# Block sums of x made early, and one VA/GA pair moved from plain chunks to block products

## The chip, the cores and the metric

The kernel runs on one core of one Trainium2 chip. The metric is the device time of one execution in microseconds. The core has TensorE (PE, matrix products into PSUM), VectorE (DVE), ScalarE (ACT), GpSimd (POOL) and SyncE (SP). ACT, POOL and SP issue the DMA transfers, most of them SP.

## The reference, cut to what matters

One decoder layer on x of 1024 positions by 1024 channels, in float32. The input projection has 56 column blocks of 128: VA and GA (8 each), XB and GB (12 each), SA and SB (8 each).

```python
h = rms_norm(x, g_mix)
z = einsum("bsd,de->bse", h, w_in) + b_in          # 1024 x 7168
va, ga, xb, gb, sa, sb = split(z)
u = va * sigmoid(ga)
u = causal_depthwise_conv(u, conv_a_w, conv_a_b)   # 31 taps
u = silu(layer_norm(u)); y_a = u @ w_a_out
v = causal_depthwise_conv(xb, conv_b_w, conv_b_b)  # 4 taps
v = rg_lru(v, ...)                                 # 16 heads, gates, scan along positions
y_b = (v * gelu(gb)) @ w_b_out
m = sigmoid(sa) * y_a + sigmoid(sb) * y_b
x = x + m @ w_o
h = rms_norm(x, g_mlp); x = x + square(relu(h @ w_1)) @ w_2
return rms_norm(x, g_final)
```

## The kernel before, in words

**Arithmetic.** Each float32 operand is split into a high part h rounded to fp32r and a low part l, the rest. A product is three matmuls: h·h, h·l and l·h. All matmuls spoken of here have a 128x128 weight and a 128x512 moving operand. There are two ways to make the parts. `split` has ACT copy h and DVE subtract to get l. `split_dma` (L64) has ACT write l = −src (L66), then POOL issues a DMA that adds src to l (L67, an accumulate), and ACT writes h = src (L68): the low part is ready when that transfer lands, and DVE has no part in it.

**Opening** (chunks 0 to 2). x is loaded, normalised and scaled into eight tiles `xc` of 128x1024, and split into `xh` and `xl`. The columns of x and of time are arranged as a 2x2 block matrix for part 2; `xc[i]` holds one half of a block.

**Part 1**, `for s in range(3, NC1)`: one chunk per step, that is one column block of `w_in` against all of x, 48 matmuls (`chunk_mm`, L724, matmul at L735). The order of the column blocks is the list `CH`: all 12 XB blocks and all 8 pairs VA, GA, 28 chunks. `w_load(s + 2)` puts the 512 KB load of a coming chunk on SP's queue, `w_parts(s + 1)` splits the next chunk's weights with `split_dma`. The chunk reads h of the weights in its first 32 matmuls and l in the last 16. Among chunk matmuls stand those of the recurrence's heads (`head_mm`). After each chunk ACT and DVE finish its column block: `xb_out` for XB, `u_out` (L583) for a VA/GA pair: ACT's sigmoid of GA and one DVE multiply of 1024 columns; `u` then feeds the 31-tap convolution. The recurrence's elementwise work comes in groups of three tiles: `scan_exp` (ACT), `scan_in` (DVE), `scan_root` (ACT), `scan_tile` (DVE, with a store to `hd`).

**Part 2** does the other column blocks in pairs (`ZPAIRS`, 14 pairs: 6 GB, 4 SA, 4 SB) by a 2x2 block scheme with seven products instead of eight. Product p of pair i is 12 matmuls (`z_mm`, L925, matmul at L933) of a left operand made from the weights (`z_lhs`, L769, out of sums of weight blocks by `z_sums`) and a right operand `xbh[p]`, `xbl[p]`. For p = 1, 2, 3 the right operand is a part of x itself; for p = 4, 5, 6, 7 it is a sum of blocks of x, split. Five of the seven left operands are split with `split_dma`, two with ACT and DVE. Products are combined in PSUM: ACT copies a bank on to another bank, and the next product adds to it. `z_bank` (L918) gives such a bank; where it says so, a first matmul into the bank comes ahead (the opening matmul, L922), for banks b and e of the first two pairs. `z_out` (L938) finishes a column block: for GB gelu and a product with the recurrence, for SA and SB a sigmoid, stored to DRAM. `zseq` is the order of all products; the loop over n takes step n of it, with left operands made four steps ahead, weight sums five ahead and weight loads (`ZL`) further ahead. `ZX` lists extra work by step.

**The sums of x.** At s = 3 eight stores write `xc` to the DRAM tensor `xu`. At s = 23 and s = 25 `x_load` (L669) reads four tiles each back on SP's queue, `x_sum` (L676) makes four differences each on DVE one chunk later, and `x_parts` (L681) splits them at s = 25 to 27 and in part 2 just ahead of step 0 and at steps 0, 2 and 4: six tiles by ACT and DVE, two (p = 5 and 4 of the first column half) by `split_dma`.

**What sets the order.** Parts 1 and 2 are under `tc.manual_schedule`: the order of each engine's instructions is the order in which the code issues them. `later` collects DVE work with a due time, and `vector_work` issues it sorted by that time and fills the spare time with convolution taps (`fill`, 0.67 us each), by a clock of planned costs (`clk["P"]`, `clk["A"]`, `clk["V"]`). SP, POOL and ACT work off their queues in order, so a transfer that waits for a tile holds up what stands behind it. Tiles come from pools with a fixed number of buffers: `tp` (tag T, 37 tiles of 128x1024) for most, `qp` (tag p, 4) for weight tiles and head tiles, `ep` (tag e) for one x tile. Part 2's last step is followed by the b stage (L1121), which needs the product of recurrence and gelu, and later by the sum over the convolution's tiles.

Of the kernel before, what the change touches and what calls it, by code (L numbers as in the profile page):

```python
# [9 lines left out]
F32 = mybir.dt.float32  # L10
# [21 lines left out]
def trunk_kernel(ctx: ExitStack, tc: tile.TileContext, x, xt_in, xt_eo, vecs, w_in, w_a_out, w_b_out,  # L32
# [87 lines left out]
    ep = stage.enter_context(tc.tile_pool(name="extra", bufs=1))  # L120
# [285 lines left out]
    xu = dp.tile([2, 4, P, S], F32, name="xu")  # L406
# [75 lines left out]
    def xb_parts(t):  # L482
        if t % 3 == 2:
            vp_[t] = tuple(qp.tile([P, S], F32R, tag="p", name=f"vt{x}{t}", bufs=4) for x in "hl")
        else:
            vp_[t] = T(f"vth{t}", F32R), T(f"vtl{t}", F32R)
# [64 lines left out]
    def scan_exp(g):  # L551
        at("A", 1.28)
        for t in range(3 * g, 3 * g + 3):
# [113 lines left out]
    xq = {}  # L667

    def x_load(c2):  # L669

        xq[c2] = {n: ep.tile([P, S], F32, tag="e", name=f"xs{n}_{c2}") if (n, c2) == (21, 0) else T(f"xs{n}_{c2}")
                  for n in (11, 12, 22, 21)}
        for n, a in xq[c2].items():
            nc.sync.dma_start(a, xu[n % 10 - 1, 2 * (n // 10 - 1) + c2])

    def x_sum(c2, ready):  # L676
        q = xq[c2]
        for n, a, b in ((11, 12, 11), (12, 22, 12), (22, 22, 11), (21, 21, 22)):
            later(ready, 1.2, nc.vector.tensor_tensor, q[n], q[a], q[b], ALU.subtract)

    def x_parts(c2, *ps):  # L681
        for p in ps:
            src = xq[c2][{6: 22, 7: 12, 5: 11, 4: 21}[p]]
            xbh[p][c2] = h = T(f"xs{p}h_{c2}", F32R)
            xbl[p][c2] = l = T(f"xs{p}l_{c2}", F32R)
            if c2 == 0 and p < 6:
                split_dma(src, h, l)
                at("A", 2.0)
            else:
                nc.scalar.activation(h, src, AF.Copy)  # L690
                later(at("A", 1.0), 1.2, nc.vector.tensor_tensor, l, src, h.bitcast(F32),
                      ALU.subtract)

    CH = [XB, VA, GA, XB + 1, XB + 2]
    for js, g in (((1,), 1), ((2,), 2), ((3,), 3), ((4, 5, 6, 7), 4)):
        CH += [c for j in js for c in (VA + j, GA + j)]
        CH += [XB + t for t in range(3 * g, min(3 * g + 3, 12))]
# [41 lines left out]
    ZPAIRS = [GB + 2 * i for i in range(6)] + [SA + 2 * i for i in range(4)]  # L739
    ZPAIRS += [SB + 2 * i for i in range(4)]  # L740
# [4 lines left out]
    def z_load(i, kk):  # L745

        zraw[i, kk] = raw = qp.tile([P, 2, 4, P], F32, tag="p", name=f"zw{i}_{kk}", bufs=4)
        c = ZPAIRS[i]
        nc.sync.dma_start(raw, w_in[c:c + 2, :, 4 * kk:4 * kk + 4, :].rearrange("m p k c -> p m k c"))
# [52 lines left out]
    HS0 = [4 + 5 * (n // 4) + n % 4 for n in range(NH)]  # L802
    head_at = {s: n for n, s in enumerate(HS0)}

    EXP = {head_slot: g for g, head_slot in enumerate(HS0[4 * g + 3] + 1 for g in range(4))}
    XL = {23: 0, 25: 1}
    XS = {25: ((x_parts, 0, 6),), 26: ((x_parts, 0, 7, 5),), 27: ((x_parts, 0, 4),)}
# [3 lines left out]
    for c2 in range(4):  # L811
        nc.sync.dma_start(xu[1, c2], xc[4 + c2])
    w_parts(3)
    with tc.manual_schedule(engines=ENGINES):
        for s in range(3, NC1):
            w_load(s + 2)
            if s in XL:
                x_load(XL[s])
# [19 lines left out]
            if before is not None:  # L838

                head_gate(before, 0, begun)  # L840
                head_mm(before, 1)
            if s > 3:
                chunk_mm(s, 18, 24)
            if new is not None:
# [20 lines left out]
            for d in range(6):  # L865
                if s - d in EXP:
                    g = EXP[s - d]
                    lag = int(g < 3)
# [9 lines left out]
                    if 3 * g <= t < 3 * g + 3 and t < 11:  # L878
                        later(rooted[t], 4.8, scan_tile, t)
            if s == NC1 - 1:  # L880
                z_get(0, z_lhs)
                z_get(1, z_lhs)
            if s - 1 in XL:
                x_sum(XL[s - 1], max((r for r, *_ in todo), default=0))
# [1221 lines left out]
```

## Time and profile before

| | |
|---|---|
| median of 3 runs | 1548.86 us (1547.82 to 1549.61) |
| profiled execution | 1549.04 us, span 1547.2 us |
| granted TensorE clock | 0.998 |
| PE busy | 1535.6 us (99%) |
| weight loads of PE busy | 1264.6 us (82%) |
| DVE busy | 1214.5 us (78%) |
| ACT busy | 903.6 us (58%) |
| POOL busy | 188.6 us (12%) |
| part 1, 33 to 360.5 us | PE busy 327.5 of 327.5, DMA share 0.60 |
| part 2, 360.5 to 630 us | PE busy 269.34 of 269.5, DMA share 0.93 |

The span runs from the first to the last instruction; the rest of an execution's time lies around it. Busy times of matmuls are modelled ends of pipelined instructions, so the difference of two starts tells more than a length. The DMA share is the mean busy share of the 16 DMA engines and can read a little over 1. In rows of a timeline the columns are start, duration, engine, line, operation, output<-inputs, and in brackets the idle time ahead with what ended it. In rows of a list of waits they are who waited for what, the total, how often, and the longest. In rows of a table by stretch they are busy time of PE, its weight loads, DVE, ACT and POOL with counts, then clock, DMA share and GB/s. In rows of DMA issues they are the tiles, the queue, the count, KB each and the median time from issue to landing.

### The profile page before, as it was taken

To read this page: it belongs to the slowest core of one execution; us is meant where nothing else is said; L and a number is where in the kernel's file an instruction comes from. 1 tells how busy PE (TensorE), PEld (TensorE's weight loads), DVE (VectorE), ACT (ScalarE), POOL (GpSimd) and SP (SyncE) were. 2 spreads that over 40 slices of the span, in tenths; PEclk is the share of its full clock that TensorE was granted. 3 is DMA by queue.
4 is the path that set the end of the run, shared out by engine and by line. 5 is a ranking of instruction groups with operands and counts; after the bars stand their busy time and mean duration, and the time that the engine had idled before them with its cause. 6 is when DMAs were issued, how large, how long until landed. Compare 5 with 4: busy or idle time off the path is not lost. (4 is left out here: it accounts for less than half of the span.)

```text
span 1547.2 us, 19086 instructions
## 1 busy us (share of the span) xinstructions
PE 1535.6 (99%) x6804; PEld 1264.6 (82%) x6804; DVE 1214.5 (78%) x1641; ACT 903.6 (58%) x1266; POOL 188.6 (12%) x226
## 2 busy tenths in 40 slices
PE   9999999999999999999999999999999999999998
PEld 7878888788888888888888887888888888888886
DVE  6999989999899983468568868765555558888897
ACT  6748677576667667435375777545444475555553
POOL 0000000002222222000022322000000001111110
PEclk9999999999999999999999999999999999999999
DMA  8653554678999889854579978523333779888852
GB/s 348 169 127 95 160 140 134 158 227 214 264 267 256 195 206 259 270 196 126 185 195 306 194 171 198 211 75 124 113 115 111 242 216 229 226 223 223 205 124 109
DMA packets 124943, 294.18 MB, mean 190 GB/s; under 512 B 12464, under 2 KB 30512, under 8 KB 124848
## 3 DMA queue, kind: packets, MB, share of 16 engines
q1 hardware_dynamic: 93312, 213.00, 40.7%
q0 software_dynamic: 31392, 79.71, 28.1%
q8 instruction: 53, 0.87, 0.2%
q14 instruction: 42, 0.34, 0.1%
q10 hardware_dynamic: 144, 0.26, 0.1%
HBM read 152.93 MB, written 58.72 MB: 137 GB/s over the span
## 5 line engine op out<-in xcount | busy, mean ns | idle before, releaser
L735 PE MATMUL z<-xh,win_h 128*128 128x512 f32 x400 | 125.0, 390 | 0.0
L735 PE MATMUL z<-xl,win_h 128*128 128x512 f32 x400 | 123.5, 390 | 0.0
L1873 DVE TENSOR_TENSOR acc<-acc,d 128x1024 f32<-128x1024 f32 x72 | 87.8, 1220 | 33.4 <-PE d L1861 32.7
L735 PE MATMUL z<-xh,win_l 128*128 128x512 f32 x400 | 99.4, 391 | 0.0
L735 PEld LDWEIGHTS z<-xh,win_l 128*128 128x128 f32 x400 | 75.2, 188 | 16.8
L735 PEld LDWEIGHTS z<-xh,win_h 128*128 128x128 f32 x400 | 75.1, 188 | 16.5 <-ACT win_h L68 0.4
L648 DVE SCALAR_TENSOR_TENSOR y<-u,vec,y 128x511 f32<-128x511 f32 (+14 forms) x120 | 88.5, 737 | 0.0
L735 PEld LDWEIGHTS z<-xl,win_h 128*128 128x128 f32 x400 | 75.1, 188 | 15.8
L648 DVE SCALAR_TENSOR_TENSOR yt<-u,vec,yt 128x511 f32<-128x511 f32 (+6 forms) x112 | 82.6, 737 | 0.0
L648 DVE SCALAR_TENSOR_TENSOR y<-yt,csum,y 128x511 f32<-128x511 f32 (+6 forms) x112 | 82.6, 737 | 0.0
L542 ACT ACTIVATE g<-rg,vec 96x1024 f32<-96x1024 f32 x32 | 35.6, 1113 | 79.6 <-PE rg L532 79.6
L1540 ACT ACTIVATE o<-s 128x512 fp32r<-128x512 f32 x58 | 34.7, 623 | 52.8 <-DVE s L1525 31.3
L67 POOL DMA_DIRECT2D win_l<-win_raw x25 | 21.6, 865 | 319.1 <-ACT win_l L66 248.4
L476 DVE SCALAR_TENSOR_TENSOR v<-xb,vec,v 128x1023 f32<-128x1023 f32 (+2 forms) x36 | 46.2, 1282 | 11.4 <-ACT v L467 10.4
L67 POOL DMA_DIRECT2D zo<-zw x42 | 36.2, 862 | 133.6 <-ACT zo L66 125.3
L1121 PE MATMUL yb<-hgl,wb_h 128*128 128x512 f32 x168 | 51.8, 390 | 0.0
L1121 PE MATMUL yb<-hgh,wb_h 128*128 128x512 f32 x168 | 51.8, 389 | 0.0
L66 ACT ACTIVATE zo<-zw 128x512 fp32r<-128x512 f32 x42 | 26.3, 626 | 30.7 <-DMA zw<-in_w_in_dram 8.7
L67 POOL DMA_DIRECT2D db_1l<-wr x7 | 6.0, 860 | 309.8 <-DMA wr<-in_w_dram 254.0
L1121 PE MATMUL yb<-hgh,wb_l 128*128 128x512 f32 x168 | 41.0, 390 | 0.0
L1085 DVE TENSOR_TENSOR o<-s,o 128x512 fp32r<-128x512 f32 x58 | 38.8, 682 | 0.0
L1121 PEld LDWEIGHTS yb<-hgh,wb_h 128*128 128x128 f32 x168 | 31.6, 188 | 6.5
(1795 smaller groups left out, 4672.9 us busy)
## 6 DMA issues: line engine op xcount, KB each, us to landing
w_raw<-in_w_dram SPq DMA_DIRECT2D x36, 512.0 KB, 5.5
fr<-fd SPq DMA_DIRECT2D x32, 512.0 KB, 5.9
wr<-in_w_dram SPq DMA_DIRECT2D x32, 512.0 KB, 6.5
zw<-in_w_in_dram SPq DMA_DIRECT2D x28, 512.0 KB, 5.9
win_raw<-in_w_in_dram SPq DMA_DIRECT2D x25, 512.0 KB, 4.1
win_l<-win_raw POOLq DMA_DIRECT2D x25, 512.0 KB, 4.5
zo<-zw POOLq DMA_DIRECT2D x42, 256.0 KB, 5.6
gates<-zg SPq DMA_DIRECT2D x32, 256.0 KB, 4.0
```

Of the source, the lines that this page charges most:

```text
L66: nc.scalar.activation(l, src, AF.Copy, scale=-1.0)
L67: nc.gpsimd.dma_start(l, src, accum_op=ALU.add)
L476: nc.vector.scalar_tensor_tensor(v[:, d:S], a[:, 0:S - d], cbw_c[:, w * 12 + t:w * 12 + t + 1], v[:, d:S], ALU.mult, ALU.add)
L542: nc.scalar.activation(a, gps.pop((n, gi))[:HD, :], AF.Sigmoid, bias=(ba_c, bx_c)[gi][:, n:n + 1])
L648: nc.vector.scalar_tensor_tensor(o[:, k:], a[:, 0:HS - k], c, o[:, k:], ALU.mult, add)
L735: nc.tensor.matmul(zps[s][:, HALVES[hf]], w[:, k, :], xw[k][part][hf], start=n == 0, stop=n == 23)
L1085: tt(l, src, h.bitcast(F32), ALU.subtract)
L1121: nc.tensor.matmul(ps[hf], a, b[:, HALVES[hf]], start=n == 0, stop=n == len(todo) - 1)
L1540: nc.scalar.activation(o[:, 0], src, AF.Copy)
L1873: tt(acc[p, q2], acc[p, q2], ps, ALU.add)
```

## The change

- The sums of x are made in place in `xc`, at s = 4 and s = 6 (`x_sum`). `x_make` at s = 5 to 7 splits those for p = 6 and 7 at once into high and low parts and has them written to the DRAM tensor `xsd` (the high part by a DMA that ACT issues, the low part by SP in `x_store`); those for p = 4 and 5 are written as they are. The eight early stores of plain x are gone; there are twelve later ones.
- `x_get` at s = 24 and 25 loads both parts for p = 6 and 7 (eight loads). `x_raw` at steps 0 and 4 of part 2 loads the sums for p = 5 and 4 (four loads), and `x_split` at steps 2, 3, 6 and 7 splits them by ACT and DVE.
- VA7 and GA7 leave part 1, which has 26 chunks (`CH` is written out, `NJ = 7`). They become the seventh of 15 pairs in part 2. `z_branch` and `z_joined` finish them by halves: ACT's sigmoid of GA in place, ACT's or DVE's sum with the bias, DVE's product.
- `z_bank` puts the opening matmul ahead of one bank only, b of the first pair.
- The first four weight loads of part 2 go to SP's queue at s = 24 of the new count, and the first two left operands are made before the last quarter of chunk 25. The scan of the last group of three tiles is spread: `scan_exp` at s = 23, `scan_in` and `scan_root` at s = 25, `scan_tile` for tiles 9, 10 and 11 at steps 1, 4 and 9 of part 2 (before: tiles 9 and 10 in part 1, 11 at step 7). New convolutions wait until step 6 instead of 2. The `v` parts of tile 9 use p buffers, and the pool `ep` is gone.

Matmuls of 128x512 before: 96 for the pair VA7, GA7, and four opening ones; after: 84 and one. DVE's 1024-wide tensor operations change by two, its 512-wide ones by eight, ACT's 1024-wide ones by seven fewer and its 512-wide by 18 more.

```diff
@@ -117,7 +117,6 @@
     wp = stage.enter_context(tc.tile_pool(name="weights", bufs=2))
-    ep = stage.enter_context(tc.tile_pool(name="extra", bufs=1))
@@ -403,7 +402,7 @@
-    xu = dp.tile([2, 4, P, S], F32, name="xu")
+    xsd = dp.tile([4, 2, 2, P, S], F32, name="xsd")
@@ -480,7 +479,7 @@
     def xb_parts(t):
-        if t % 3 == 2:
+        if t in (2, 5, 8, 9):
             vp_[t] = tuple(qp.tile([P, S], F32R, tag="p", name=f"vt{x}{t}", bufs=4) for x in "hl")
@@ -548,9 +547,10 @@
-    def scan_exp(g):
-        at("A", 1.28)
-        for t in range(3 * g, 3 * g + 3):
+    def scan_exp(g, part=range(3)):
+        if 0 in part:
+            at("A", 1.28)
+        for t in (3 * g + n for n in part):
             r = gate[0, t]
@@ -664,37 +664,46 @@
-    xq = {}
-
-    def x_load(c2):
-
-        xq[c2] = {n: ep.tile([P, S], F32, tag="e", name=f"xs{n}_{c2}") if (n, c2) == (21, 0) else T(f"xs{n}_{c2}")
-                  for n in (11, 12, 22, 21)}
-        for n, a in xq[c2].items():
-            nc.sync.dma_start(a, xu[n % 10 - 1, 2 * (n // 10 - 1) + c2])
-
-    def x_sum(c2, ready):
-        q = xq[c2]
-        for n, a, b in ((11, 12, 11), (12, 22, 12), (22, 22, 11), (21, 21, 22)):
-            later(ready, 1.2, nc.vector.tensor_tensor, q[n], q[a], q[b], ALU.subtract)
-
-    def x_parts(c2, *ps):
-        for p in ps:
-            src = xq[c2][{6: 22, 7: 12, 5: 11, 4: 21}[p]]
-            xbh[p][c2] = h = T(f"xs{p}h_{c2}", F32R)
-            xbl[p][c2] = l = T(f"xs{p}l_{c2}", F32R)
-            if c2 == 0 and p < 6:
-                split_dma(src, h, l)
-                at("A", 2.0)
-            else:
-                nc.scalar.activation(h, src, AF.Copy)
-                later(at("A", 1.0), 1.2, nc.vector.tensor_tensor, l, src, h.bitcast(F32),
-                      ALU.subtract)
-
-    CH = [XB, VA, GA, XB + 1, XB + 2]
-    for js, g in (((1,), 1), ((2,), 2), ((3,), 3), ((4, 5, 6, 7), 4)):
-        CH += [c for j in js for c in (VA + j, GA + j)]
-        CH += [XB + t for t in range(3 * g, min(3 * g + 3, 12))]
+    def x_sum(c2):
+        q11, q12, q22, q21 = (xc[i + c2] for i in (0, 4, 6, 2))
+        for o, a, b in ((q11, q12, q11), (q12, q22, q12), (q22, q22, q11), (q21, q21, q22)):
+            later(clk["P"] - 7, 1.2, nc.vector.tensor_tensor, o, a, b, ALU.subtract)
+
+    def x_make(c2, p):
+        src = xc[{5: 0, 7: 4, 6: 6, 4: 2}[p] + c2]
+        if p in RAW:
+            stored.append((xsd[p - 4, c2, 0], src))
+            return
+        h, l = (T(f"xs{p}{n}_{c2}", F32R) for n in "hl")
+        nc.scalar.activation(h, src, AF.Copy)
+        nc.scalar.dma_start(xsd[p - 4, c2, 0], h.bitcast(F32))
+        later(at("A", 1.1), 1.2, nc.vector.tensor_tensor, l, src, h.bitcast(F32), ALU.subtract)
+        stored.append((xsd[p - 4, c2, 1], l.bitcast(F32)))
+
+    stored = []
+
+    def x_store():
+        for a in stored:
+            nc.sync.dma_start(*a)
+        stored.clear()
+
+    def x_get(c2, p):
+        for n, a in enumerate((xbh, xbl)):
+            a[p][c2] = T(f"xb{p}{'hl'[n]}_{c2}", F32R)
+            nc.sync.dma_start(a[p][c2].bitcast(F32), xsd[p - 4, c2, n])
+
+    def x_raw(c2, p):
+        xbl[p][c2] = T(f"xb{p}l_{c2}", F32R)
+        nc.sync.dma_start(xbl[p][c2].bitcast(F32), xsd[p - 4, c2, 0])
+
+    def x_split(c2, p):
+        xbh[p][c2], l = T(f"xb{p}h_{c2}", F32R), xbl[p][c2]
+        nc.scalar.activation(xbh[p][c2], l.bitcast(F32), AF.Copy)
+        later(at("A", 1.06), 1.2, nc.vector.tensor_tensor, l, l.bitcast(F32), xbh[p][c2].bitcast(F32),
+              ALU.subtract)
+
+    NJ = 7
+    CH = [XB + 0, VA + 0, GA + 0, XB + 1, XB + 2, VA + 1, GA + 1, XB + 3, XB + 4, XB + 5, VA + 2, GA + 2, XB + 6, XB + 7, XB + 8, VA + 3, GA + 3, XB + 9, XB + 10, XB + 11, VA + 4, GA + 4, VA + 5, GA + 5, VA + 6, GA + 6]
     NC1 = len(CH)
@@ -736,8 +745,8 @@
-    ZPAIRS = [GB + 2 * i for i in range(6)] + [SA + 2 * i for i in range(4)]
-    ZPAIRS += [SB + 2 * i for i in range(4)]
+    ZPAIRS = [(c, c + 1) for c in range(GB, SB + 8, 2)]
+    ZPAIRS[6:6] = [(VA + j, GA + j) for j in range(NJ, 8)]
     NZ = len(ZPAIRS)
@@ -745,8 +754,8 @@
         zraw[i, kk] = raw = qp.tile([P, 2, 4, P], F32, tag="p", name=f"zw{i}_{kk}", bufs=4)
-        c = ZPAIRS[i]
-        nc.sync.dma_start(raw, w_in[c:c + 2, :, 4 * kk:4 * kk + 4, :].rearrange("m p k c -> p m k c"))
+        c, d = ZPAIRS[i]
+        nc.sync.dma_start(raw, w_in[c:d + 1:d - c, :, 4 * kk:4 * kk + 4, :].rearrange("m p k c -> p m k c"))
@@ -799,23 +808,22 @@
                mybir.EngineType.SP, mybir.EngineType.Pool}
-    HS0 = [4 + 5 * (n // 4) + n % 4 for n in range(NH)]
+    HS0 = [(4, 9, 14, 19)[n // 4] + n % 4 for n in range(NH)]
     head_at = {s: n for n, s in enumerate(HS0)}
-    EXP = {head_slot: g for g, head_slot in enumerate(HS0[4 * g + 3] + 1 for g in range(4))}
-    XL = {23: 0, 25: 1}
-    XS = {25: ((x_parts, 0, 6),), 26: ((x_parts, 0, 7, 5),), 27: ((x_parts, 0, 4),)}
+    EXP = {head_slot: g for g, head_slot in enumerate(HS0[4 * g + 3] + 1 for g in range(3))}
+    RAW = (4, 5)
+    XS = {4: ((x_sum, 0),), 5: ((x_make, 0, 5), (x_make, 0, 7)), 6: ((x_make, 0, 6), (x_make, 0, 4), (x_sum, 1)),
+          7: tuple((x_make, 1, p) for p in (5, 7, 6, 4)),
+          NC1 - 3: ((scan_exp, 3),), NC1 - 2: ((x_get, 0, 6), (x_get, 1, 6)),
+          NC1 - 1: ((scan_in, 0, 9, 10, 11), (scan_root, 3), (x_get, 0, 7), (x_get, 1, 7))}
     w_load(3)
...
     w_load(4)
-    for c2 in range(4):
-        nc.sync.dma_start(xu[1, c2], xc[4 + c2])
     w_parts(3)
...
             w_load(s + 2)
-            if s in XL:
-                x_load(XL[s])
             taps["hold"] = s > NC1 - 4
@@ -839,8 +847,12 @@
                 head_mm(before, 1)
+            if s == NC1 - 1:
+                z_get(0, z_lhs)
+                z_get(1, z_lhs)
             if s > 3:
                 chunk_mm(s, 18, 24)
+            x_store()
             if new is not None:
@@ -865,7 +877,7 @@
                     g = EXP[s - d]
-                    lag = int(g < 3)
+                    lag = 1
                     if d == 0:
@@ -875,21 +887,13 @@
                     t = 3 * g + d - 2 - lag
-                    if 3 * g <= t < 3 * g + 3 and t < 11:
+                    if 3 * g <= t < 3 * g + 3 and t < 10:
                         later(rooted[t], 4.8, scan_tile, t)
-            if s == NC1 - 1:
-                z_get(0, z_lhs)
-                z_get(1, z_lhs)
-            if s - 1 in XL:
-                x_sum(XL[s - 1], max((r for r, *_ in todo), default=0))
+            if s == NC1 - 2:
+                for i in range(4):
+                    z_load(i // 2, i % 2)
             for f, *a in XS.get(s, ()):
                 f(*a)
-            if s == NC1 - 3:
-                for i in range(4):
-                    z_load(i // 2, i % 2)
-            if s == 3:
-                for c2 in range(4):
-                    nc.sync.dma_start(xu[0, c2], xc[c2])
             vector_work(clk["P"] - 0.7)
@@ -917,7 +921,7 @@
         zb[i, b] = t = zp.tile([P, HS], F32, tag="z", name=f"z{i}{b}")
-        if i < 2 and b in "be":
+        if i == 0 and b == "b":
@@ -936,9 +940,11 @@
     def z_out(i, m_, hf, src, name):
-        ci = ZPAIRS[i] + m_
+        ci = ZPAIRS[i][m_]
         bias = bin_c[:, ci:ci + 1]
-        if ci < SA:
+        if ci < XB:
+            z_branch(ci, hf, src, bias)
+        elif ci < SA:
             t = ci - GB
@@ -957,11 +963,37 @@
+    zu, zg = {}, {}
+
+    def z_branch(ci, hf, src, bias):
+        j = ci % GA
+        if j not in zu:
+            zu[j] = T(f"u{j}")
+        d, g = halved(zu[j], hf), src.rearrange("p (n o) -> p o n", o=2)
+        if ci >= GA:
+            zg[j, hf] = g
+            nc.scalar.activation(src, src, AF.Sigmoid, bias=bias)
+            ready = at("A", 0.62)
+            if hf == 0:
+                later(ready, 0.63, nc.vector.tensor_tensor, d, d, g, ALU.mult)
+                z_joined(j)
+        elif hf == 0:
+            nc.scalar.activation(d, g, AF.Identity, bias=bias)
+            at("A", 0.62)
+        else:
+            later(0, 0.68, nc.vector.scalar_tensor_tensor, d, g, bias, zg.pop((j, hf)), ALU.add, ALU.mult)
+            z_joined(j)
+
+    def z_joined(j):
+        if j in ut:
+            fresh.append(j)
+        ut[j] = zu[j]
+
...
     def z_h(i, m_, hf):
-        t = ZPAIRS[i] + m_ - GB
-        if t < 12:
+        t = ZPAIRS[i][m_] - GB
+        if 0 <= t < 12:
             hb[t, hf] = h = EV(f"hb{t}_{hf}")
@@ -994,7 +1026,9 @@
-    ZX = {0: ((x_parts, 1, 7),), 7: ((later, 0, 4.8, scan_tile, 11),), 2: ((x_parts, 1, 5),), 4: ((x_parts, 1, 4),)}
+    ZX = {0: ((x_raw, 0, 5), (x_raw, 1, 5)), 1: ((later, 0, 4.8, scan_tile, 9),), 2: ((x_split, 0, 5),), 3: ((x_split, 1, 5),),
+          4: ((later, 0, 4.8, scan_tile, 10), (x_raw, 0, 4), (x_raw, 1, 4)), 6: ((x_split, 0, 4),), 7: ((x_split, 1, 4),),
+          9: ((later, 0, 4.8, scan_tile, 11),)}
     H_AT = {2: (0, 0), 5: (1, 1), 3: (0, 1), 4: (1, 0)}
@@ -1037,8 +1071,7 @@
         z_get(3, z_lhs)
-        u_out(7, zps[NC1 - 2], zps[NC1 - 1])
-        x_parts(1, 6)
+        u_out(NJ - 1, zps[NC1 - 2], zps[NC1 - 1])
         vector_work(clk["V"])
@@ -1047,7 +1080,7 @@
                     f(*a)
-            taps["hold"] = n < 2
+            taps["hold"] = n < 6
             if n >= 20 and n % 6 == 2:
...
             clk["A"], clk["V"] = max(clk["A"], clk["P"] + 0.5), max(clk["V"], clk["P"] - 2)
```

## The prediction

> **What bounds the kernel now.** I read the page's busy shares first, then the list of waits of TensorE (PE), then its timeline around the last chunks of part 1, then the DMA views of the same stretch.
>
> ```profile
> span 1547.2 us, 19086 instructions
> ...
> PE 1535.6 (99%) x6804; PEld 1264.6 (82%) x6804; DVE 1214.5 (78%) x1641; ACT 903.6 (58%) x1266; POOL 188.6 (12%) x226
> ```
>
> ```profile
> PE gu4a L1297 <- ACT u_late L1351: 1.6, 1, 1.6
> ...
> PE z4e L933 <- DMA zo<-zs: 0.2, 1, 0.2
> ```
>
> PE is busy 99% of the span, and between the first chunks and the b stage its list of waits holds one entry, 0.2 us. So the time is the number of matmuls times their spacing, as long as nothing makes PE wait. The spacing follows from starts:
>
> ```profile
> 338.81 0.39 PE L735 MATMUL z<-xh,win_h 128*128 128x512 f32 x1
> 349.69 0.39 PE L735 MATMUL z<-xh,win_h 128*128 128x512 f32 x1
> 360.57 0.39 PE L933 MATMUL z0a<-xh,zo 128*128 128x512 f32 x1
> 363.29 0.39 PE L922 MATMUL z0b<-xh 128*128 128x512 f32 x1
> 363.52 0.39 PE L933 MATMUL z1a<-xh,zo 128*128 128x512 f32 x1
> ```
>
> Two chunks of 48 matmuls take 349.69 − 338.81 and 360.57 − 349.69, 10.88 us each: 0.2267 us per matmul, though one is listed as 0.39 long (they overlap). A block product of 12 takes 363.29 − 360.57 = 2.72 us, the same spacing, and the opening matmul 363.52 − 363.29 = 0.23. Weight loads need 82% of the span and hide. Beside this the Trainium skill (Perfetto Trace Analysis, section Identifying the Most-Contended Engine) says that matmul busy time is a poor measure of how close PE is to its limit, and that the share of weight loads is a better one. Taken alone, 82% would leave PE a fifth in hand and 15 fewer matmuls would bring next to nothing; the even 0.2267 us speaks against that reading here.
>
> **The change part by part.**
>
> *PE.* Removed: the last chunk pair, VA7 and GA7, 2 × 48 matmuls = 2 × 10.88 = 21.76 us. Added: a fifteenth pair in part 2, 7 products × 2.72 = 19.04. Removed: three of four opening matmuls, 3 × 0.2267 = 0.68. Together 15 matmuls, 21.76 − 19.04 + 0.68 = **3.40 us less**. Nothing covers PE, so all of it lies on the path, and any new wait of PE is paid in full.
>
> *DVE and ACT.* Their work is hidden by PE's, so it costs nothing until an operand is late.
>
> ```profile
> L453 DVE TENSOR_TENSOR xs<-xs,xs x8: 1217/1224/1227, 327.1 to 348.8; 128x1024 f32<-128x1024 f32 x8
> L690 ACT ACTIVATE xs6h<-xs x2: 1043/1044/1046, 335.1 to 362.5; 128x1024 fp32r<-128x1024 f32 x2
> ...
> L453 DVE TENSOR_TENSOR xs7l<-xs,xs7h x2: 1218/1222/1227, 350.0 to 365.6; 128x1024 fp32r<-128x1024 f32 x2
> ```
>
> The eight sums (8 × 1.22 = 9.8 us of DVE) move from 327–349 to s = 4 and 6; the split of p = 7 and 6 goes to s = 5 to 7 (4 × 1.04 ACT, 4 × 1.22 DVE), that of p = 5 and 4 stays in part 2 (steps 2, 3, 6, 7). Two splits that an accumulating DMA did become DVE subtractions (+2.4 us). The new pair adds ten operations on 512 columns (0.69 us each, as the row of L655 below) and drops one on 1024 columns. All of it displaces convolution taps. After the convolutions DVE has room:
>
> ```profile
> 575.50 0.69 DVE L655 TENSOR_TENSOR y<-y,yt 128x511 f32<-128x511 f32 x1
> ```
>
> ```profile
> 580.00:600.00 20.00, 20.00 (x90) 16.58 (x89) 6.53 (x10) 12.37 (x23) 5.20 (x6) 1.00 0.99 233
> 600.00:620.00 20.00, 20.00 (x90) 16.57 (x89) 9.73 (x11) 16.93 (x26) 5.16 (x6) 1.00 1.02 288
> ```
>
> The last convolution tile ends at 576, and in the 40 us that follow DVE is busy 16.3. The convolution of channel block 7 starts later, since its input now comes from pair 6 instead of a chunk; it has those 24 idle us, and its result is wanted after part 2. I cost it at zero; if the cover went, the cost would be what exceeds 24 us.
>
> *DMA.* This is where a wait can come from. Before: 8 stores of the scaled x, 8 loads of 512 KB, two accumulates of 512 KB (xs5l, xs4l). After: 12 stores early; loads of p = 6 and 7 (8 × 512 KB) with the four weight loads of the first z pairs put on SP's queue at s = 24 and 25; 4 loads at z steps 0 and 4. Two chunks' weights with two accumulates leave part 1 and come back as two weight loads and five accumulates of 256 KB in part 2. The four early stores of high parts sit on ACT's own queue; ACT waits on nothing for them and its issue is the only cost, far from any tight place. The row that can hurt is the low part of the last chunk's weights, which POOL accumulates and PE reads in the last third of the chunk:
>
> ```profile
> 327.07 0.86 POOL L67 DMA_DIRECT2D win_l<-win_raw  x1 [19.26 <-ACT win_l L66]
> ```
>
> ```profile
> 335.18 0.39 PE L735 MATMUL z<-xh,win_l 128*128 128x512 f32 x1
> ```
>
> ```profile
> win_l<-win_raw POOLq DMA_DIRECT2D x1, 512.0 KB, 4.5
> ```
>
> ```profile
> xs<-xu SPq DMA_DIRECT2D x8, 512.0 KB, 8.1
> ...
> win_l<-win_raw POOLq DMA_DIRECT2D x3, 512.0 KB, 10.6
> ...
> zw<-in_w_in_dram SPq DMA_DIRECT2D x2, 512.0 KB, 17.3
> ```
>
> ```profile
> DMA to landing us min/median/max: 4.5/9.3/11.0
> ```
>
> The first three are POOL's and PE's timelines and the DMA issues in 325–332, the last two the issues in 300–335 and the win_l group in 300–360. The chunk at s = 25 keeps its place (ahead of it run as many chunks as before, so its first matmul should again start near 327.8). Its accumulate was issued at 327.07, took 4.5 us and was wanted 8.1 us after issue. The same accumulate took up to 11.0 with many 512 KB loads outstanding. After the change it is the last chunk, and the loads run ahead of it:
>
> ```profile
> 305.00:310.00 5.00, 5.00 (x24) 4.14 (x23) 4.86 (x5) 2.60 (x3) 0.86 (x1) 1.00 1.03 322
> 310.00:315.00 5.00, 5.00 (x24) 3.94 (x23) 5.00 (x8) 0.83 (x1) 0.00 (x0) 1.00 1.02 261
> 315.00:320.00 5.00, 5.00 (x24) 4.12 (x23) 5.00 (x9) 4.92 (x5) 0.00 (x0) 1.00 0.85 302
> 320.00:325.00 5.00, 5.00 (x24) 4.15 (x23) 4.47 (x7) 4.92 (x5) 0.00 (x0) 1.00 0.15 59
> 325.00:330.00 5.00, 5.00 (x23) 3.80 (x22) 4.07 (x4) 4.97 (x5) 0.86 (x1) 1.00 0.55 147
> ```
>
> In the full slices a 512 KB transfer takes 0.524 MB / 295 GB/s = 1.8 us (mean of 305–320). SP's queue holds about twelve of them between 309 and the accumulate (last chunk weights, one head store, four zw, six of the x parts): 309 + 12 × 1.8 = 331, so the quiet gap at 320–325 is filled and the accumulate shares its first 4 us. Bounds of the wait: 4.5 us to land gives none, 11.0 gives 11.0 − 8.1 = 2.9 us. The median 9.3 gives 1.2; since the crowd ends halfway through I take half of that, **0.6 us**. Beside this the Trainium skill (DMA: Bandwidth & Descriptors, section Queues, rings and completion order) says that each DMA engine takes turns between queue rows packet by packet. By that an accumulate on its own row would at most double, an estimate of 9.0 us and a wait of 0.9; the measured 10.6 beside SP's loads is more than double the quiet 4.5, so the trace puts the price above the rule's.
>
> *The first block products.* Their left operands are accumulated too:
>
> ```profile
> L67 POOL DMA_DIRECT2D zo<-zw x40: 851/860/886, 360.3 to 618.2; - x40
> ...
> DMA to landing us min/median/max: 3.3/6.1/9.4
> ```
>
> ```profile
> 366.24 0.39 PE L922 MATMUL z1b<-xh 128*128 128x512 f32 x1
> ```
>
> The third product's operand is issued at 360.3 and read at 366.24 + 0.23 = 366.5: 6.2 us. At the median 6.1 nothing waits, at 9.4 it is 3.2 us. What eases it: the zw loads, which took 17.3 us, are now issued some 20 us earlier, relative to PE about as early, in a gap. What tightens it: four x loads, two stores of head tiles and the splits of p = 5 and 4 fall into steps 0 to 7. Bounds 0 and 3.2, I take **0.6 us**, nearer to zero because the median row shows none. The third and fourth pair wait behind the same SP queue (a head store that waits for DVE stands ahead of zw of pair 2); cost zero, since in the densest stretch of all
>
> ```profile
> 465.61 0.73 PE L933 MATMUL z4e<-xh,zo 128*128 128x512 f32 x2 [0.16 <-DMA zo<-zs]
> ```
>
> is the only wait. Where the last chunk's stall goes, the first z operands get that much more lead.
>
> *Sum.* −3.40 + 0.6 + 0.6 = −2.2 us. The profiled execution took 1549.04 (span 1547.2 and 1.84 around it), 0.18 above the median of 1548.86: 1546.84 against it, **1546.7** against the median.
>
> **The rivals.**
>
> *Full gain.* Every accumulate lands in time, as the 4.5 us row and the median of 6.1 suggest: 1548.86 − 3.40 = 1545.5. Against it: 10.6 beside loads. Chance 0.29. If the 0.2 us wait at z4e goes as well, about 1545.2.
>
> *Gain eaten.* Waits of 3.4 to 6.4 us, for instance both upper bounds, 2.9 + 3.2: −3.4 + 6.1 = +2.7, 1551.6. At the low end 1548.9. Chance 0.08.
>
> *DMA becomes the bound from s = 24 to the third pair* (the other side). Part 1 is 21.8 us shorter, so that much DMA time is gone. Demand falls by two loads (3.6 us) and four accumulates (counted twice, as read and add, 4 × 3.6 = 14.4), and rises by four x loads (7.2): net 10.8. So the stretch is 11 us tighter. It had idle DMA of 5 × (0.85 + 0.45) = 6.5 us in 320–330, and some more up to 340 and after 370. If that does not suffice, accumulates stay at 9 to 11 us for several steps: 2.9 at the last chunk and 3.2 at two places of the first pairs, 9.3 in all, 1548.86 − 3.4 + 9.3 = 1554.8. It decides the sign when new waits exceed 3.4, and shows as slower beyond 3.4 + 3.1 = 6.5. Against it: shares above 1.0 further on, with only 0.2 us of wait. Chance 0.20.
>
> *The sums don't leave.* The x sums could delay heads or taps at s = 4 to 7; ACT and DVE have no wait there that PE sees, and I leave it inside the forecast's case.
>
> **How the numbers follow.** 0.2% is 3.1 us, about what a measurement of this kernel can tell from no change. The forecast (waits of 0.4 to 3.4, 1545.9 to 1548.9) has 0.43. Faster by over 0.2% needs waits under 0.3 us, the full gain: 0.29. Within 0.2%: 0.43 + 0.08 = 0.51. Slower: 0.20. The range goes from 1545.0 (full gain and the small waits of before gone) to 1552.0, which takes in both upper bounds and leaves out about half of the DMA case and a little below.
>
> **What would show it.** Right: 15 matmuls fewer on PE, z0a starting near 338.8, part 2 ending 3 us earlier than before at an unchanged 0.2267 us; waits on win_l at the last chunk or on zo in the first pairs, together about 1.2 us. Wrong: a wait over 3 us at the last chunk, waits on zo in more than two products of pairs 0 to 2, ACT waiting for an x load at steps 2 to 7 with PE behind it, or a wait at the b stage for DVE.

## The result and the profile after

| | before | after |
|---|---|---|
| median | 1548.89 us (8 runs) | 1552.95 us (8 runs, 1550.97 to 1554.42) |
| ratio | 1 | 1.0026, 95% interval 1.0015 to 1.0037 |
| profiled execution | 1549.04 us, span 1547.2 | 1554.42 us, span 1552.6 |

The changed kernel is 4.1 us slower, where 2.2 us less was forecast. The profiled execution is its slowest, 1.5 us above the median, so sizes from its trace lie at the upper end.

The page's busy line and PE's list of waits, after (who waited for what, total, times, longest):

```profile
PE 1535.2 (99%) x6789; PEld 1262.2 (81%) x6789; DVE 1223.0 (79%) x1652; ACT 905.2 (58%) x1276; POOL 189.9 (12%) x227
```

```profile
PE z0a L937 <- DVE u L452: 3.4, 1, 3.4
PE z14e L937 <- ACT zc L1014: 1.7, 1, 1.7
...
PE z5b L937 <- DMA zo<-zs: 0.8, 1, 0.8
PE z2e L937 <- DMA zo<-zs: 0.8, 1, 0.8
PE z4a L937 <- DMA zo<-zw: 0.6, 1, 0.6
PE yb L1154 <- DVE hgl L452: 0.5, 1, 0.5
PE gu4a L1330 <- ACT u_late L1384: 0.4, 1, 0.4
```

The 15 matmuls are gone (6804 to 6789). The busy line hardly moves; the list of waits does. Three new groups stand in it: one long wait of the very first block product, on DVE; three on accumulated left operands at 410 to 445 us; two at the end of part 2 (z14e, and yb at its seam with the b stage).

**The first group.** PE, DVE and ACT after, around the start of part 2:

```profile
337.73 1.07 PE L744 MATMUL z<-xh,win_l 128*128 128x512 f32 x4
342.15 0.77 PE L937 MATMUL z0a<-xh,zo 128*128 128x512 f32 x1 [3.36 <-DVE u L452]
342.72 0.63 PE L937 MATMUL z0a<-xl,zo 128*128 128x512 f32 x1
343.14 1.05 PE L937 MATMUL z0a<-xh,zo 128*128 128x512 f32 x2
...
345.45 0.63 PE L937 MATMUL z0a<-xh,zo 128*128 128x512 f32 x2
```

```profile
339.52 0.69 DVE L452 TENSOR_TENSOR zs<-zs,zw 128x512 f32<-128x512 f32 x1
...
340.73 1.28 DVE L452 SCALAR_TENSOR_TENSOR u<-z,vec,u 128x1024 f32<-128x1024 f32 x1
```

```profile
338.83 1.11 ACT L587 ACTIVATE u<-z,vec 128x1024 f32<-128x1024 f32 x1 [1.53 <-PE z L744]
```

z0a does not wait for an operand but for its PSUM bank. In both kernels the program gives z0a the bank that chunk 24 had. Chunk 24 is VA6, and VA6 is read by the multiply of `u_out`, which also needs GA6. Before, GA6 was chunk 25 and two more chunks followed, so the bank was long free. After, chunk 25 is the last chunk: ACT takes the sigmoid of GA6 from 338.83 to 339.94, DVE ends three sums of weight blocks first and multiplies at 340.73, and PE stands still until 342.15. A second loss follows, which the table by stretch shows (the columns as before: PE, weight loads, DVE, ACT, POOL, granted clock, DMA share, GB/s):

```profile
338.70:342.00 3.30, 0.09 (x1) 0.00 (x0) 3.27 (x6) 2.26 (x3) 0.83 (x1) 0.96 0.76 209
342.00:345.00 3.00, 2.85 (x7) 2.30 (x8) 2.90 (x5) 0.00 (x0) 0.03 (x1) 0.50 0.83 214
```

For 3 us after the wait the granted clock is 0.50. The eight intervals from the start at 342.15 to that at 345.45 take 3.3 us, where 8 × 0.2267 = 1.8 is usual: 1.5 us more. The place costs about 5 us in this execution.

**The second group** are left operands that stand in POOL's queue behind an accumulate into `ysum` (experiment 4). They stand so in the kernel before too, at the same place of part 2: the first accumulate there is issued 54.7 us behind the start of z0a before (415.3) and 55.7 us after (397.9). What differs is that these accumulates take longer to land (8.5 to 9.6 us before, 10.4 to 10.7 after). The waits are not the same in every execution: in the traces of `e1_bank` and `e5_fill`, whose edits leave the accumulates where they are, the three together are 0 and 0.3 us, against 2.2 here. Why is not shown.

**The third group** begins with convolutions that come later. The stores of their results (eight, first and last start), before and after, and the last accumulate into `ysum` with the loads of `hg` around it (median us to landing), before 596 to 630, after 600 to 634:

```profile
L656 SPq DMA_DIRECT2D yd<-y x8: 319/341/434, 108.0 to 576.2; - x8
```

```profile
L656 SPq DMA_DIRECT2D yd<-y x8: 326/366/716, 128.3 to 600.7; - x8
```

```profile
hg<-hgd SPq DMA_DIRECT2D x11, 512.0 KB, 6.6
...
ysum<-yd POOLq DMA_DIRECT2D x1, 512.0 KB, 6.1
```

```profile
hg<-hgd SPq DMA_DIRECT2D x10, 512.0 KB, 8.6
...
ysum<-yd POOLq DMA_DIRECT2D x1, 512.0 KB, 9.4
```

The first convolution already ends 20 us later (128.3 against 108.0), since the sums of x fall on DVE at s = 4 to 7; the last one 24.5 us later. Its accumulate, which was issued at 594.8, now comes at 610.3, among the loads of `hg`. These land later, ACT waits for them in its order, copies z14e late, and PE waits 1.7 us.

### The profile page after: what moved, and what is told of

The parts are those of the page before. It is cut to its first block, busy times and chain, and to the rows that moved or that the text cites. A ratio compares the mean times of both kernels' runs of the same rounds, so it can differ in the third digit from the quotient of the medians.

```text
span 1552.6 us, 19102 instructions
## 1 busy us (share of the span) xinstructions
PE 1535.2 (99%) x6789; PEld 1262.2 (81%) x6789; DVE 1223.0 (79%) x1652; ACT 905.2 (58%) x1276; POOL 189.9 (12%) x227
## 4 chain that ended last, share of the span: by engine, by line
PE 86%; DMA 5%; DVE 4%; ACT 2%; issue 1%; SPq 1%; POOL 0%; DVEq 0%; POOLq 0%; ACTq 0%
PE d L1894 15%; PE z L744 11%; PE yb L1154 8%; PE e L2011 3%; PE keep L1894 2%; PE z L257 2%; DMA hg<-hgd 1%; DMA zo<-zs 1%; DVE y L648 1%; PE rg L531 1%; PE rg L529 1%; PE rg L530 1%; DMA w_raw<-in_w_dram 1%; DMA zo<-zw 1%; DMA xb6h<-xsd 1%
## 5 line engine op out<-in xcount | busy, mean ns | idle before, releaser
L744 PE MATMUL z<-xh,win_h 128*128 128x512 f32 x368 | 115.0, 390 | 0.0
L744 PE MATMUL z<-xl,win_h 128*128 128x512 f32 x368 | 113.5, 389 | 0.0
L744 PE MATMUL z<-xh,win_l 128*128 128x512 f32 x368 | 91.8, 391 | 0.0
L744 PEld LDWEIGHTS z<-xh,win_l 128*128 128x128 f32 x368 | 69.1, 188 | 15.7
L744 PEld LDWEIGHTS z<-xh,win_h 128*128 128x128 f32 x368 | 69.0, 188 | 15.3 <-ACT win_h L68 0.4
L744 PEld LDWEIGHTS z<-xl,win_h 128*128 128x128 f32 x368 | 69.1, 188 | 14.6
L1154 PEld LDWEIGHTS yb<-hgl,wb_h 128*128 128x128 f32 x168 | 31.5, 188 | 6.5
```

What stands on the lines that cost most here:

```text
L744: nc.tensor.matmul(zps[s][:, HALVES[hf]], w[:, k, :], xw[k][part][hf], start=n == 0, stop=n == 23)
L1154: nc.tensor.matmul(ps[hf], a, b[:, HALVES[hf]], start=n == 0, stop=n == len(todo) - 1)
```

## The experiments

All numbers are medians in us beside those of the kernel before measured together with it, and the ratio with its interval. The kernel before itself moved between 1548.06 and 1548.89 from one experiment to the next, so two edits are compared by their ratios. The interval of such a difference is about 0.0014 to either side (2.2 us) with the changed kernel's 1.0026, and about 0.0013 (2 us) between two of the others. Each profile is of one execution, which need not be near the median. Steps count the products of part 2.

**1. Another bank for z0a** (`e1_bank`). One-column memsets by DVE take chunk 24's two banks first.

```diff
+        nc.vector.memset(zp.tile([P, HS], F32, tag="z", name="zd0")[:, 0:1], 0.0)   # ahead of step 0
         z_h(0, 0, 0)
...
     def z_bank(i, b):
+        if (i, b) == (1, "a"):
+            nc.vector.memset(zp.tile([P, HS], F32, tag="z", name="zd")[:, 0:1], 0.0)
```

> The changed kernel, with the first block product put into a PSUM bank that chunk 23 or a head used (two one-column DVE memsets take the banks of chunk 24 first). Theory (bank): z0a waited 3.36 us because its bank was that of VA6's chunk, the last but one, which DVE reads only after the last chunk; and the granted clock then stood at 0.61 for the first matmuls. Both go: z0a starts near 338.8 instead of 342.15, its 12 matmuls take 2.72 us instead of 4.2, and the time falls by 3.5 + 1.5 = 5.0 us to about 1548.0. Rival (DMA): the operands of the first products are late as well, so a wait on zo or on an x part takes the place, and less than 2 us is gained (above 1551).

Measured 1548.61 beside 1548.30, ratio 1.0009 (1.0000 to 1.0018). PE after this edit:

```profile
338.04 0.62 PE L744 MATMUL z<-xh,win_l 128*128 128x512 f32 x2
338.50 0.39 PE L939 MATMUL z0a<-xh,zo 128*128 128x512 f32 x1
338.72 0.39 PE L939 MATMUL z0a<-xl,zo 128*128 128x512 f32 x1
```

z0a follows the last chunk without a gap at 0.22 us spacing. By the medians 4.3 of the expected 5.0 us came, by the ratios 2.6 (0.0017 × 1549); the runs spread over 6.6 us. The profiled execution is the fastest of them (1545.59), and in it the waits at z2e, z4a and z5b are gone as well and that at z14e is 0.3, so its time is not the bank's doing alone. Operands were ready, so the rival at this place falls.

**2. The same clash put into the kernel before** (`e7_before_clash`). Six such memsets ahead of step 0 leave z0a a bank of chunk 26, which is VA7 there.

```diff
+        for n in range(6):
+            nc.vector.memset(zp.tile([P, HS], F32, tag="z", name=f"zd{n}")[:, 0:1], 0.0)
```

> The kernel before, with z0a put into the PSUM bank of chunk 26 (VA7) by six one-column DVE memsets that take the banks ahead of it. Theory (bank): the wait appears in the kernel before as well: z0a waits for DVE's multiply of u7 some 2 to 3.4 us, the granted clock falls, and the time rises by 3.5 to 5.0 us to 1552 to 1554. Rival: the wait in the changed kernel has to do with its later DVE work and not with the bank; here under 1 us is lost.

Measured 1552.53 beside 1548.07, ratio 1.0032 (1.0021 to 1.0043). Its list of waits has the line that the changed kernel has:

```profile
PE z0a L933 <- DVE u L453: 3.0, 1, 3.0
```

So the bank alone makes a kernel 4.5 us slower, with nothing else of the change in it; the memsets also give the later products other banks. That is as much as the whole change cost. The profiled execution is the fastest of six (1551.46), with 3.0 us of wait and the usual spacing behind it; where the others lost the rest was not traced.

**3. PE kept at work in the wait** (`e5_fill`).

```diff
+            if s == NC1 - 1:
+                spare = PS("held", "ps2")
+                for _ in range(15):
+                    nc.tensor.matmul(spare[:, 0:HS], xh[0][0][:, 0:P], xh[0][0][:, 0:HS], start=True, stop=True)
```

> The changed kernel, with 15 matmuls of 128x512 into an unused bank (results dropped) behind the last chunk, so that PE works through the 3.4 us in which z0a waits. Theory (clock): of the 5.0 us at that place 1.5 come from a granted clock of 0.61 after the idle time; with PE kept at work z0a still starts near 342.2, but its 12 matmuls take 2.7 us instead of 4.2, and the time is about 1551.4. Rival: the first matmuls are slow because their operands come late; their spacing stays at 0.43 us and the time at 1553.

Measured 1550.54 beside 1548.07, ratio 1.0016 (1.0007 to 1.0025): 15 matmuls more, and 2.4 us less by the medians, 1.5 by the ratios (0.0010, inside the interval of such a difference).

```profile
338.70 3.56 PE L859 MATMUL held<-xh 128*128 128x512 f32 x15
342.22 0.47 PE L941 MATMUL z0a<-xh,zo 128*128 128x512 f32 x1
342.52 0.39 PE L941 MATMUL z0a<-xl,zo 128*128 128x512 f32 x1
```

z0a starts at the same 342.2, but now at the usual spacing. The slow matmuls came from the clock, not from operands: in the traces that were read, the slow spacing stands with a lowered clock and the usual spacing with 1.00. That the filling keeps the clock up is not shown by this one trace, since the clock also stayed at 1.00 in one execution with the idle time (`e12_tail_only`, last section).

**4. Later accumulates into `ysum`** (`e3_mid`: from step 50 on instead of 20).

```diff
-            if n >= 20 and n % 6 == 2:
+            if n >= 50 and n % 6 == 2:
```

> The changed kernel, with no accumulate into ysum before step 50 of part 2 (before: from step 20 on). Theory: the waits of PE at z2e, z4a and z5b (0.8, 0.6, 0.8 us, 2.6 us more than the usual spacing) come from left operands queued behind a 512 KB ysum accumulate of 10.5 us; all three go and the time falls by about 2.6 to 1550.3. Rival: the loads of hb, the stores of hgd and the head tiles crowd the DMA engines there anyway; waits of the same size stay at steps 24 to 40, and the time stays within 0.8 of 1553.

Measured 1550.51 beside 1548.30, ratio 1.0015 (1.0006 to 1.0024): 2.4 us less than the changed kernel by the medians, 1.7 by the ratios, which is inside the interval of such a difference. The waits at z2e, z4a and z5b are gone; one of 0.6 us at z3a is new. Since `e1_bank` and `e5_fill` lost these waits without this edit, it is not shown that the accumulates alone make them.

**5. The eighth accumulate** (`e2_last`, `e12_tail_only`).

```diff
-            if n >= 20 and n % 6 == 2:
-                sum_up(clk["P"], 1)
+            if n >= 20 and n % 6 == 2 and summed and summed[0][1] < 7 or n == L + 1:   # e12; e2 without "or ..." and with the old next line
+                sum_up(math.inf if n > L else clk["P"], 1)
```

> The changed kernel, with the last of the eight accumulates into ysum issued after the last left operand of part 2 instead of at 610. Theory: that accumulate, which the later convolution of block 7 has pushed in among the loads of hg, makes hg land late, ACT waits for hg, copies z14e late, and PE waits 1.7 us for it and 0.5 for hgl; both go, together 2.5 us with the gaps around them, about 1550.5. Rival (order): with 15 pairs the last products simply come too close together; the wait at z14e stays and the time is within 0.7 of 1553.

Measured 1551.83 beside 1548.30, ratio 1.0027 (1.0016 to 1.0039). The edit did not do what its expectation says: left to the next stage, the accumulate was placed at 603.4, earlier than before the edit (610.3), and met the first loads of `hg`. The wait at z14e went, one of 1.8 us at z13e came. It says nothing for or against the theory.

> The changed kernel with the eighth accumulate into ysum behind the last left operand of part 2, and no other edit. Theory: the waits at z14e and hgl (2.5 us with the gaps) go, and the time falls from 1552.95 to about 1550.7. Rival: the loads of hg are late for another reason (the DMA engines are full there in any case); less than 1 us is gained.

Here it stands behind the last left operand in POOL's queue, at 621.1, still among the loads of `hg`. Measured 1552.11 beside 1548.06, ratio 1.0026 (1.0015 to 1.0036). The wait at z14e is gone from the trace and hgl waits 0.3 instead of 0.5, but the time is the changed kernel's within the interval. By itself this wait was worth less than the 2.2 us expected. The rival's figure (under 1 us) came true: the loads of `hg` land no sooner (7.5 us at the median of the twelve, 7.1 in the changed kernel), though z14e no longer waits.

**6. The edits together** (`e4_all`, `e8_tail`).

> All three edits at once: another bank for z0a, ysum from step 50 on, its last accumulate behind part 2. Theory: nothing of the waits of part 2 is left, and the 15 matmuls that are gone show: 1548.9 - 3.4 = 1545.5, or 1545.0 if the 0.4 us that the kernel before lost at z4e goes as well. Rival: the waits removed come back elsewhere, since operands have 9 us of lead and the DMA engines are as busy as before: 1547 to 1550.

These are the edits of 1, 4 and `e2_last`. Measured 1547.65 beside 1548.30, ratio 0.9998 (0.9990 to 1.0007), with the eighth accumulate misplaced as in `e2_last`, 2.0 us of wait at z13e and 1.3 at z2a.

> The kernel with all three edits again, but with the last accumulate into ysum now truly behind the last left operand of part 2 in POOL's queue (in the two runs before it stood ahead of the loads of hg, 7 us earlier than in the changed kernel, not later). Theory: hg0 then lands about 6 us after its issue instead of 11, ACT reaches the left operand of product (13, 3) in time, the wait of 2.0 us at z13e goes, and the time is about 1545.6. Rival: the loads of hg crowd the queue by themselves; a wait of over 1 us at z13e or z14e stays and the time is 1547 to 1548.

These are the edits of 1, 4 and `e12_tail_only`. Measured 1546.40 beside 1548.07, ratio 0.9989 (0.9980 to 0.9998). PE's list of waits of `e8_tail`:

```profile
PE z0e L939 <- ACT zc L1016: 0.5, 1, 0.5
PE yb L1158 <- DVE hgl L452: 0.5, 1, 0.5
PE gu4a L1334 <- ACT u_late L1388: 0.3, 1, 0.3
PE z2a L939 <- DMA zo<-zw: 0.2, 1, 0.2
```

Nothing over 0.5 us is left in part 2 of this execution, and the kernel is faster than the one before by 1.7 us; the interval just leaves out no change.

**7. The pair left in part 1** (`e6_pair_stays`, and with the late accumulates `e13_stays_tail`).

```diff
-    NJ = 7
+    NJ = 8
-    CH = [..., VA + 6, GA + 6]
+    CH = [..., VA + 6, GA + 6, VA + 7, GA + 7]
```

> The changed kernel with VA7 and GA7 back in part 1 (28 chunks, 14 pairs): what is left of the change is the early sums of x, their stores and twelve loads, the moved scans and one opening matmul instead of four. Theory (pair): the losses come from the moved pair, by the bank and by the later convolution of block 7; here z0a's bank was last read two chunks earlier, there is no wait at z0a or z13e, and the time is that of before less 0.7, plus up to 1 us for tighter first products: 1548 to 1549. Rival (sums of x): the twelve loads and the moved scans are what costs; waits on zo in the first pairs of over 2 us, above 1550.

Measured 1550.34 beside 1548.07, ratio 1.0017 (1.0008 to 1.0026). No wait at z0a, as expected, but no 1548 either: the early sums of x with their stores, loads and scans cost by themselves. The theory that the losses come from the pair alone falls, and so does its rival's picture of 2 us of waits on zo: the trace has 0.2 us of that and 1.4 us at the b stage, where `hg` comes late. The convolutions end later still than in the changed kernel: the last store of a result is issued at 608.9, against 576.2 before.

> The kernel with VA7 and GA7 back in part 1 (1550.3 us, 2.3 more than before and with no wait at z0a), and the accumulates into ysum from step 50 on, the eighth behind the last left operand. Theory (late sums): the 14 tile operations on DVE that the early sums of x put into part 1 delay all convolutions, the last accumulates meet the first products and the loads of hg, and that is the whole loss; without it the kernel is 0.7 us faster than the one before, 1547.3. Rival (loads): the twelve loads of x parts and the moved scans cost it; the time stays above 1549.5.

Measured 1549.59 beside 1548.81, ratio 1.0008 (0.9999 to 1.0016). (DVE's tile operations that the early sums put into part 1 are twelve, eight sums and four low parts, and not 14.) The result lies between the two expectations: 1.4 us less than with the accumulates in place (1.0017 − 1.0008, inside the interval of such a difference), and 1.9 us more than the kernel with one opening matmul and nothing else (experiment 8: 1.0008 − 0.9996). The trace shows where such a loss can sit, in waits that the kernel before and `e10_one_opening` don't have:

```profile
PE yb L1154 <- DVE hgl L452: 1.1, 2, 0.5
PE z1f L937 <- DMA zo<-zw: 0.5, 1, 0.5
...
PE yb L1154 <- ACT hgh L1057: 0.2, 1, 0.2
```

1.3 us of it is at the b stage: loads of `hg` take 7.8 us to landing here and 6.3 in `e10_one_opening`, ACT and DVE split them later, and PE waits for the parts. The last accumulate is issued at 619.9 here and at 619.1 in `e6_pair_stays`, so that part of the edit hardly moved anything; what makes `hg` late stays open.

**8. One opening matmul in the kernel before** (`e10_one_opening`).

```diff
-        if i < 2 and b in "be":
+        if i == 0 and b == "b":
```

> The kernel before with one opening matmul instead of four, nothing else. Theory: PE is dense there, so three matmuls are 0.7 us: 1547.4 beside 1548.1. Rival: the copies into those banks, or the operands, wait anyway, and nothing is gained.

Measured 1547.25 beside 1548.06, ratio 0.9996 (0.9988 to 1.0005). The median moves by 0.8 us as expected, inside the interval.

**9. Smaller steps on `e8_tail`** (`e9_store`, `e11_hold`, `e14_best`).

```diff
-        nc.sync.dma_start(hd[t], i)                        # e9, e14: tiles 9, 10, 11 by scan_store at steps 5, 8, 13
-            taps["hold"] = n < 6
+            taps["hold"] = n < 2                           # e11, e14
```

> As the kernel with the three edits and the accumulate at the end, with the stores of head tiles 9, 10 and 11 put on SP's queue at steps 5, 8 and 13 instead of 1, 4 and 9, so that weight loads of pairs 2 and 3 no longer stand behind a store that waits for DVE's scan. Theory: zw of pair 2 lands 2 to 5 us earlier, ACT makes the left operands of products (1, 4), (2, 6) and (2, 2) 9 us ahead instead of 4.6 to 6.7, and the waits of up to 1.3 us there go: 0.5 to 1 us less than 1546.4. Rival: the accumulates are slow there (7 to 9 us) by the load alone; no change within 0.4.

> As the kernel with the three edits and the accumulate at the end, with new convolutions held until step 2 of part 2 (as before) instead of 6. Theory: DVE stood idle for part of those 11 us, the convolutions end up to 8 us earlier than 594.5, and it changes nothing in the time, since the last accumulate is out of the way: 1546.4 within 0.5. Rival: the splits of p = 5 and the scans come later by the taps, PE waits for xb5 parts in product (0, 5), and the time rises by 1 us or more.

> All edits that gained or cost nothing at once: another bank for z0a, ysum from step 50 on with its last accumulate at the end, stores of head tiles 9 to 11 later on SP's queue, new convolutions from step 2. Theory: what is left of 15 matmuls is 3.4 us, less about 1 us of waits on accumulates in the first pairs: 1545.8, faster than the kernel before. Rival: the waits of the first pairs grow with the taps let in at step 2; 1546.4 or more.

Measured 1546.05 (ratio 0.9990, 0.9981 to 0.9999) and 1546.33 (0.9990, 0.9981 to 0.9999), both beside 1548.06, and 1547.56 beside 1548.81 (0.9991, 0.9982 to 1.0000). None can be told from `e8_tail`. In `e14_best` the waits of the first pairs grew to 2.7 us in its trace, as its rival said. But `e11_hold` lets the same taps in, and its trace has 0.2 us there, so the taps are not shown to be the cause.

## Why the prediction was wrong, point by point

**PE, −3.40 us: right.** The pair is worth what was worked out: with the same late accumulates, the pair in part 2 and a free bank give a ratio of 0.9989, the pair in part 1 gives 1.0008, a difference of 2.9 us, give or take 2, for the 2.72 predicted. The three opening matmuls gave 0.8 by the median for 0.68, inside the interval.

**"The first block products": the step that failed.** It asked when their left operands land and put 0.6 us, with 3.2 as the upper bound. It never asked which PSUM bank the first of them writes and who reads that bank last. Taking two chunks off the end of part 1 moves VA6 from fourth and GA6 from third last to the last two places, while the bank assignment stays. The price was 3.4 us of wait and, with the clock, up to 5 us, and z0a started at 342.15, where the prediction named 338.8. Of the operands themselves the prediction was about right: without the bank wait none is late at z0a, and the waits on left operands in pairs 0 to 3 are 0.2 us in `e8_tail`, 0.4 in `e1_bank`, and at most 1.5 in the other kernels with a free bank (`e14_best`).

**"DVE and ACT ... I cost it at zero": failed too.** The cover was computed as 24 idle us behind the convolutions, with the words that their result is wanted after part 2. The early sums make all convolutions later, the first by 20 us; with the pair left in part 1 (`e6_pair_stays`) the last ends 33 us later, more than the cover. And what is done later has to share the end of part 2 with the loads of `hg`. The early sums with all that belongs to them cost about 3 us (1.0017 in `e6_pair_stays` against 0.9996 in `e10_one_opening`), of which 1.4 us stand in the trace as waits on `hg` at the b stage. The prediction had named a wait at the b stage for DVE as a sign of being wrong, and it is there (0.5 us in the changed kernel). That the delay of the convolutions is what costs, and not the loads or the moved scans, is argued and not shown.

The accumulates in the middle of part 2 are another matter, since they stand at the same place in both kernels. Their slower landing could be seen in the views, 8.5 to 9.6 us before, and after (390 to 460 us)

```profile
DMA to landing us min/median/max: 10.4/10.5/10.7
```

Moving them off is worth 1.7 us by the ratios in `e3_mid`, no more than the interval.

**The last chunk's accumulate, 0.6 us: no wait at all.** It was issued at 326.92, landed 4.6 us later and was wanted at 335.0. The term that was mis-sized is the rate at which the crowd ahead of it is worked off: 295 GB/s, or 1.8 us a transfer, was taken from the kernel before; after, from 315 to 325 the same loads ran at over 400 (1.3 us each), so that they were through by 327 and not 331: the DMA share is 0.42 from 326 to 327 and 0.03 in the us after. The gap at 320 to 325 was filled, as predicted.

```profile
315.00:320.00 5.00, 5.00 (x24) 4.12 (x23) 5.00 (x9) 4.91 (x6) 0.00 (x0) 1.00 1.04 401
320.00:325.00 5.00, 5.00 (x24) 4.14 (x23) 1.70 (x3) 4.94 (x5) 0.00 (x0) 1.00 1.03 411
```

```profile
win_l<-win_raw POOLq DMA_DIRECT2D x1, 512.0 KB, 4.6
```

The Trainium skill (DMA: Bandwidth & Descriptors, section Queues, rings and completion order), by whose turn-taking 9.0 us had been estimated, is not tested by it, since the crowd had gone.

**The rivals.** The sign is that of "DMA becomes the bound", and its time (1554.8) is not far off, but that is luck: of its 9.3 us of waits for accumulates the trace has 2.2, none of them at the last chunk, and the largest single loss is not a DMA. In the sum, 3.4 gained stand against a bank loss (2.6 by ratios to 4.3 by medians in `e1_bank`, 4.5 put into the kernel before) and about 3 us that the x sums cost. With the openings counted once that gives +2 to +4, and 4.1 was measured. The waits depend on one another, as `e1_bank` and `e5_fill` show, so this is a rough account. What makes the x sums cost that much stays open; neither the twelve loads nor the moved scans were tried by themselves.

## What to carry to other kernels

When work is cut from the end of a stage, list for each resource that the next stage takes over, PSUM banks above all, who its last reader was and how far from the end; shortening a stage can put the slowest reader last. A tile that an off-path engine finishes later is not free until its transfers are followed to their landing, because they join queues that the critical engine reads from. And a wait of PE may cost more than itself: here 3.4 us cost up to 5, by the clock.

## What the runs showed of the hardware

After the same 3.35 to 3.36 us of idle at z0a the granted clock fell in three of four executions (to 0.50 in the changed kernel and `e3_mid`, to 0.75 in `e2_last`, over 342 to 345), and stayed at 1.00 in `e12_tail_only`; nor did it fall after 3.0 us in `e7_before_clash`:

```profile
342.00:345.00 3.00, 2.33 (x10) 1.99 (x11) 2.90 (x5) 0.00 (x0) 0.54 (x1) 1.00 0.84 241
```

(the row of `e12_tail_only`). So the loss of about 1.5 us comes in some executions and not in others. Whether it makes the spread of the runs (3.5 us after, 2.0 before) is not shown: `e1_bank` has no such idle time and spreads over 6.6.
